# A two-layer transformer with a hybrid block on Trainium2: who splits weights and activations in the first stage

## The chip, the cores and the metric

One core of a Trainium2 chip. The metric is the device time of one execution in microseconds, as a median over runs. The engines are TensorE (PE; its weight loads are PEld), VectorE (DVE), ScalarE (ACT), GpSimd (POOL) and SyncE (SP), whose queue issues the loads and stores.

## The reference, cut to what matters

Two transformer layers, a gated mixer in the first and attention in the second, followed by a third block (mLSTM and sparse attention). Sequence 512, width 1024, float32. The change lies in the very first stage:

```python
c_act = silu(c)
mod = c_act @ ada_w[0] + ada_b[0]
sh_m, sc_m = mod[:1024], mod[1024:2048]
h = rms_norm(x, pre_mix_g[0]) * (1 + sc_m) + sh_m
z = gelu(h @ a_w_in[0] + a_b_in[0])
u, v = split(z, 2)
```

Beside it, `p @ w_ple` (the embedding for the end of the program) is computed here too.

## The kernel before

**Products in three parts.** Every matrix product is made of three passes of PE. An operand f is split into a high part (f rounded to the matmul's format) and a low part (f minus the high part), and `mm3` (L415) adds high x high, high x low and low x high: L416, L417 and L418. So each weight of 128 x 1024 that is loaded into a `raw` buffer (four of them) needs two operations in `wsplit` (L274): ACT makes the high part `whi` (L279), DVE or POOL the low part `wlo` (L282). The argument `share=1` gives the low part to POOL; without it DVE has it; `share=3` gives POOL every third of all splits, by a counter.

**The first stage** (from L595) works through the eight blocks of 128 columns of the normed x, k = 0 to 7. Its order on ACT, DVE, PE and SP is the order in which the code is written (a manual schedule); where the text below says that something stands behind something else on an engine, it can't pass it. `prep(k)` does:

- `mods(k)` (L705): two products of DVE with `cact` (silu of c, copied to all rows), each over a loaded 128 x 1024 block `d` of the modulation weights with a sum into one column of `modc` (`ada`, L302). Three operations on single columns follow: the bias on the shift (L708), the scale plus bias plus 1 (L709), and times the norm's gain, into `g0` (L710).
- the split of one weight: on even k a chunk of `w_v` (low part on POOL), on k = 1 and 3 one of `w_u` (low part on DVE).
- `to_T(k)` (L372): four transposes on PE (L384), then ACT applies scale and shift from PSUM into `t` (L407), then DVE casts `t` to the high part of h (L408) and subtracts for the low part (L409).

`products(k)` follows on PE: 12 matmuls of h against `w_v`'s chunk k/2 into four accumulators, and matmuls of `w_u` for two blocks, with some of them caught up when a block begins. `prep(k+1)` is written ahead of `products(k)`.

**Ahead of it**, the start-up: silu of c on ACT (L670), PE's copy of it to all rows (L683) and DVE's copy into `cact` (L685), the splits of `w_pl`, the squares and norms of x (L668, L656 to L664), and the embedding's products with their copies (L649, L651). The loads stand on SP in the order of the code: `crow` (which is c) first, then `pT`, `w_pl`, x, and the modulation blocks with the first `w_v` and `w_u` between them.

**Behind it** the accumulators are evacuated (`ev_v`, L764 to L766), and `gemm_b` goes on with the other three groups of `w_v`, with modulation columns for later stages in between.

## Time and profile before

| | |
|---|---|
| median of 3 runs | 1910.1 us (1907.51 to 1917.22) |
| the profiled execution | 1910.77 us, span 1908.9 us |
| PE busy | 1832.5 us, 96% of the span |
| DVE busy | 1130.9 us, 59% |
| ACT busy | 792.2 us, 41% |
| POOL busy | 375.9 us, 20% |
| granted PE clock, mean | 0.983 |

Times in the trace are microseconds from the start of the span. A row of the timeline has the start, the duration, the engine, the line, what is written and read, and in brackets how long the engine was idle before it and who ended that. In the windows view the columns are the stretch, its length, the busy time of PE, PEld, DVE, ACT and POOL with the count of instructions, the granted PE clock as a share of 2.4 GHz, the share of DMA time and the rate.

### The profile page before, as it was taken

What the parts mean: (1) busy time and instruction counts of PE and PEld (TensorE: products, weight loads), DVE (VectorE), ACT (ScalarE), POOL (GpSimd) and SP (SyncE); (2) the same over time, 40 slices, a digit from 0 to 9 for tenths busy, and PEclk for the clock granted to TensorE, in tenths of its full rate; (3) what the DMA queues carried; (4) which work ended last, traced back from release to release, by engine and by line L of the source; (5) the groups of instructions that cost most, each with busy time, mean ns of one, the idle gap of its engine ahead of it and who ended that gap; (6) DMA issues with size and microseconds to landing.
All of it is one profiled execution on the core that took longest, in us unless ns stands there. A gap on an engine that the chain in (4) does not pass through costs nothing. (4 is left out here: it accounts for less than half of the span.)

```text
span 1908.9 us, 23835 instructions
## 1 busy us (share of the span) xinstructions
PE 1832.5 (96%) x8688; PEld 1514.8 (79%) x8688; DVE 1130.9 (59%) x2132; ACT 792.2 (41%) x1395; POOL 375.9 (20%) x216
## 2 busy tenths in 40 slices
PE   8899989999999999799998999999989999999998
PEld 5788877888888877587777888888878888888887
DVE  7879844677772256439876433232267978846534
ACT  5334324423232245448764422222246246455334
POOL 2100122222220012344323111100020363031011
PEclk9999999999999999899998999999989999999999
DMA  8684752477773444855533222222434744332522
GB/s 336 235 280 134 238 207 83 158 266 271 249 253 107 136 144 145 265 177 157 185 100 111 92 97 99 97 98 103 144 116 134 231 143 135 105 105 89 192 90 100
DMA packets 109647, 305.75 MB, mean 160 GB/s; under 512 B 12277, under 2 KB 15133, under 8 KB 109530
## 3 DMA queue, kind: packets, MB, share of 16 engines
q1 hardware_dynamic: 109530, 304.23, 47.8%
q8 instruction: 69, 1.13, 0.2%
q14 instruction: 48, 0.39, 0.1%
HBM read 269.50 MB, written 37.30 MB: 161 GB/s over the span
## 5 line engine op out<-in xcount | busy, mean ns | idle before, releaser
L279 ACT ACTIVATE whi<-raw 128x1024 fp32r<-128x1024 f32 x293 | 309.9, 1059 | 672.0 <-PE acc L418 295.9
L282 POOL TENSOR_TENSOR wlo<-raw,whi 128x1024 fp32r<-128x1024 f32 x124 | 305.2, 2465 | 1348.5 <-ACT whi L279 1062.2
L417 PE MATMUL acc<-h,whi 128*128 128x512 f32 (+1 forms) x1112 | 417.3, 375 | 10.4 <-DVE h L409 10.2
L416 PE MATMUL acc<-h,whi 128*128 128x512 f32 (+1 forms) x1112 | 417.6, 376 | 5.8 <-DVE h L408 5.2
L418 PE MATMUL acc<-h,wlo 128*128 128x512 f32 (+1 forms) x1112 | 416.0, 374 | 0.6 <-POOL wlo L282 0.6
L282 DVE TENSOR_TENSOR wlo<-raw,whi 128x1024 fp32r<-128x1024 f32 x169 | 214.4, 1271 | 299.2 <-ACT whi L279 294.7
L416 PE MATMUL acc<-whi,h 128*128 128x512 f32 x608 | 241.4, 398 | 19.5 <-ACT whi L279 12.2
L417 PEld LDWEIGHTS acc<-h,whi 128*128 128x128 f32 x1112 | 212.3, 191 | 48.2 <-DVE h L409 12.7
L416 PEld LDWEIGHTS acc<-h,whi 128*128 128x128 f32 x1112 | 212.4, 191 | 42.1 <-DVE h L408 6.0
L417 PE MATMUL acc<-wlo,h 128*128 128x512 f32 x608 | 240.0, 395 | 4.8 <-DVE wlo L282 3.3
L418 PEld LDWEIGHTS acc<-h,wlo 128*128 128x128 f32 x1112 | 212.4, 191 | 37.2 <-POOL wlo L282 1.0
L418 PE MATMUL acc<-whi,h 128*128 128x512 f32 x608 | 240.2, 395 | 0.0
L416 PE MATMUL acc<-whi,s 128*128 128x512 f32 (+1 forms) x488 | 190.5, 390 | 0.7 <-DVE t L1305 0.7
L302 DVE SCALAR_TENSOR_TENSOR raw<-raw,cact 128x1024 f32<-128x1024 f32 x96 | 146.7, 1535 | 74.8 <-DMA raw<-in_ada 68.2
L417 PE MATMUL acc<-wlo,s 128*128 128x512 f32 (+1 forms) x488 | 190.7, 391 | 0.0
L418 PE MATMUL acc<-whi,s 128*128 128x512 f32 (+1 forms) x488 | 190.2, 390 | 0.0
L416 PEld LDWEIGHTS acc<-whi,h 128*128 128x128 f32 x608 | 115.2, 190 | 44.3 <-ACT whi L279 12.6
L417 PEld LDWEIGHTS acc<-wlo,h 128*128 128x128 f32 x608 | 115.2, 190 | 29.2 <-DVE wlo L282 4.1
L418 PEld LDWEIGHTS acc<-whi,h 128*128 128x128 f32 x608 | 115.2, 190 | 26.0 <-DVE h L409 3.0
L416 PEld LDWEIGHTS acc<-whi,s 128*128 128x128 f32 x488 | 91.7, 188 | 20.0 <-DVE t L1305 1.1
L417 PEld LDWEIGHTS acc<-wlo,s 128*128 128x128 f32 x488 | 91.7, 188 | 18.8
L418 PEld LDWEIGHTS acc<-whi,s 128*128 128x128 f32 x488 | 91.7, 188 | 18.8
(349 smaller groups left out, 2395.4 us busy)
## 6 DMA issues: line engine op xcount, KB each, us to landing
raw<-in_ada SPq DMA_DIRECT2D x96, 512.0 KB, 3.7
raw<-in_w_gu SPq DMA_DIRECT2D x88, 512.0 KB, 3.7
raw<-in_w_dn SPq DMA_DIRECT2D x44, 512.0 KB, 3.2
scr<-t SPq DMA_DIRECT2D x72, 256.0 KB, 3.8
raw<-in_w_o SPq DMA_DIRECT2D x20, 512.0 KB, 3.3
row<-scr SPq DMA_DIRECT2D x36, 256.0 KB, 3.3
d<-in_ada SPq DMA_DIRECT2D x16, 512.0 KB, 5.5
raw<-in_w_v SPq DMA_DIRECT2D x16, 512.0 KB, 5.1
```

The source lines that it names most:

```text
L279: S_.activation(hi[:, 0:n], raw[:, 0:n], AF.Copy)
L282: e.tensor_sub(lo[:, 0:n], raw[:, 0:n], hi[:, 0:n].bitcast(F32))
L302: V.scalar_tensor_tensor(raw, raw, 1.0, cact[0], ALU.mult, ALU.mult, accum_out=modc[:, col:col + 1])
L416: PE.matmul(out, lh, rh, start=start, stop=False)
L417: PE.matmul(out, lh, rl, start=False, stop=False)
L418: PE.matmul(out, ll, rh, start=False, stop=stop)
```

## The change

In the first stage, the high part of h is made by ACT in a second pass over the same PSUM tile (`twice`, L408 and L409 of the changed code), and DVE only subtracts (L412 there). All low parts of `w_v` go to DVE (no `share` any more). A weight is split behind h (`take(k)`) and one step earlier in the count of k than it is used: `w_v`'s chunk 0 ahead of everything, `w_u` in the steps of h0 and h2, the chunks of `w_v` in those of h1, h3 and h5. The operations on columns are two instead of three: 1 plus the bias of the scale is added once for all eight columns (`ab1`, L705 there), then one operation makes `g0` (L711) and one the shift (L712). And `crow` is loaded as the fourth load instead of the first.

```diff
@@ -369,7 +369,7 @@
             for h in range(2):
                 V.tensor_scalar_mul(out[h], xr[h], ss[:, 2:3])
 
-        def to_T(ts, xn, g, sh, hi, lo, js=range(KD), spill=None):
+        def to_T(ts, xn, g, sh, hi, lo, js=range(KD), spill=None, twice=False):
 
 
             n = len(ts) * P
@@ -405,7 +405,10 @@
                     S_.activation(fj, src, AF.Copy, scale=g[:, j:j + 1])
                 else:
                     S_.activation(fj, src, AF.Identity, scale=g[:, j:j + 1], bias=sh[:, j:j + 1])
-                V.tensor_copy(hi[j][:, c], fj)
+                if twice:
+                    S_.activation(hi[j][:, c], src, AF.Identity, scale=g[:, j:j + 1], bias=sh[:, j:j + 1])
+                else:
+                    V.tensor_copy(hi[j][:, c], fj)
                 V.tensor_sub(lo[j][:, c], fj, hi[j][:, c].bitcast(F32))
 
         def hpair():
@@ -608,13 +611,12 @@
             EVA = (0, 0)
 
             crow = L2()[0:1, :]
-            nc.sync.dma_start(crow, a["crow"])
             pf = [L(), L()]
-            wpl = []
+            wpl = [load_w(a["w_pl"][0, 0])]
             for k in range(2):
                 nc.sync.dma_start(pf[k], a["pT"][k])
-            for k in range(2):
-                wpl.append(load_w(a["w_pl"][k, 0]))
+            nc.sync.dma_start(crow, a["crow"])
+            wpl.append(load_w(a["w_pl"][1, 0]))
             xn = {}
             for t in range(NT):
                 xn[t] = [L(), L()]
@@ -699,29 +701,36 @@
                     bt = L()[0:8, 0:n]
                     V.tensor_copy(bt, pt[0:8, 0:n])
                     bts.append((bt, c0, n))
-                g0 = newg()
+                g0, ab1 = newg(), newg()
+                V.tensor_scalar_add(ab1, vc("adab", 8, 8), 1.0)
 
 
                 def mods(j, loads):
                     for col, raw in loads:
                         ada(col, raw)
+                    V.scalar_tensor_tensor(g0[:, j:j + 1], modc[:, 8 + j:9 + j], ab1[:, j:j + 1], vc("pmg0", j), ALU.add, ALU.mult)
                     V.tensor_add(modc[:, j:j + 1], modc[:, j:j + 1], vc("adab", j))
-                    V.scalar_tensor_tensor(g0[:, j:j + 1], modc[:, 8 + j:9 + j], 1.0, vc("adab", 8 + j), ALU.add, ALU.add)
-                    V.tensor_mul(g0[:, j:j + 1], g0[:, j:j + 1], vc("pmg0", j))
                 wv, uw, uaccs = {}, {}, []
                 early_w = []
 
+                def take(k):
+
+                    if k % 2:
+                        c = k // 2 + 1
+                        if c < KD // 2:
+                            wv[c] = wsplit(a["w_v"][0, c], raw=raws.get(2 * c))
+                    elif k // 2 < NU:
+                        uw[k // 2] = wsplit(a["w_u"][k // 2], alloc=L2, raw=raws.get(k + 1))
+
                 def prep(k):
+                    if k == 0:
+                        wv[0] = wsplit(a["w_v"][0, 0], raw=raws[0])
                     mods(k, ada0[k] if k in ada0 else [ada_load(col, L2() if k % 2 < ND else None) for col in (8 + k, k)])
-                    c = k // 2
-                    if k % 2 == 0:
-                        wv[c] = wsplit(a["w_v"][0, c], share=1, raw=raws.get(k))
-                    elif c < NU:
-                        uw[c] = wsplit(a["w_u"][c], alloc=L2, raw=raws.get(k))
                     if k == 0:
                         embed(0, 1)
                         embed(1, 1)
-                    to_T(range(NT), xn, g0, modc, *h, js=(k,))
+                    to_T(range(NT), xn, g0, modc, *h, js=(k,), twice=True)
+                    take(k)
                     if k == 0:
                         embed(2, 1)
                         embed(3, 1)
```

The order on DVE at the step that leads to h0 and in the first period behind it, before (`h_96` is h's high part for k = 0, `h_104` its low part, `d_148` to `d_156` are modulation blocks, `gcol` holds `g0`):

```order
L302 SCALAR_TENSOR_TENSOR d_148,modc<-d_148,cact_194 128x1024
L302 SCALAR_TENSOR_TENSOR d_150,modc<-d_150,cact_194 128x1024
L708 TENSOR_TENSOR modc<-modc,vecs 128x1
L709 SCALAR_TENSOR_TENSOR gcol<-modc,vecs 128x1
L710 TENSOR_TENSOR gcol<-gcol,vecs 128x1
L408 CAST h_96<-t_307 128x512
L409 TENSOR_TENSOR h_104<-t_307,h_96 128x512
L302 SCALAR_TENSOR_TENSOR d_154,modc<-d_154,cact_194 128x1024
L302 SCALAR_TENSOR_TENSOR d_156,modc<-d_156,cact_194 128x1024
L708 TENSOR_TENSOR modc<-modc,vecs 128x1
L709 SCALAR_TENSOR_TENSOR gcol<-modc,vecs 128x1
L710 TENSOR_TENSOR gcol<-gcol,vecs 128x1
```

and in the changed kernel (there `gcol` also holds `ab1`):

```order
L705 TENSOR_SCALAR gcol<-vecs 128x8
L282 TENSOR_TENSOR wlo_277<-raw_152,whi_276 128x1024
L302 SCALAR_TENSOR_TENSOR d_148,modc<-d_148,cact_194 128x1024
L302 SCALAR_TENSOR_TENSOR d_150,modc<-d_150,cact_194 128x1024
L711 SCALAR_TENSOR_TENSOR gcol<-modc,gcol,vecs 128x1
L712 TENSOR_TENSOR modc<-modc,vecs 128x1
L412 TENSOR_TENSOR h_104<-t_307,h_96 128x512
L282 TENSOR_TENSOR d_312<-raw_158,d_311 128x1024
L302 SCALAR_TENSOR_TENSOR d_154,modc<-d_154,cact_194 128x1024
L302 SCALAR_TENSOR_TENSOR d_156,modc<-d_156,cact_194 128x1024
L711 SCALAR_TENSOR_TENSOR gcol<-modc,gcol,vecs 128x1
L712 TENSOR_TENSOR modc<-modc,vecs 128x1
```

The low part of `w_v` (`wlo_277`) now stands ahead of the first product, the cast is gone, and the low part of `w_u` (`d_312`) stands between h0's low part and the next two products.

The order on ACT around h5 (L407 makes `t`, L279 a weight's high part; `raw_526` and `raw_494` are `w_v`'s last chunk, `raw_613`, `raw_615`, `raw_606` and `raw_608` the first two weights of the next stage), before:

```order
L407 ACTIVATE t_449<-tp_444,modc,gcol 128x512
L407 ACTIVATE t_495<-tp_490,modc,gcol 128x512
L279 ACTIVATE whi_528<-raw_526 128x1024
L407 ACTIVATE t_537<-tp_532,modc,gcol 128x512
L279 ACTIVATE whi_656<-raw_613 128x1024
L279 ACTIVATE whi_686<-raw_615 128x1024
L407 ACTIVATE t_573<-tp_568,modc,gcol 128x512
```

and in the changed kernel:

```order
L407 ACTIVATE t_445<-tp_440,modc,gcol 128x512
L409 ACTIVATE h_100<-tp_440,modc,gcol 128x512
L407 ACTIVATE t_490<-tp_485,modc,gcol 128x512
L409 ACTIVATE h_101<-tp_485,modc,gcol 128x512
L279 ACTIVATE whi_496<-raw_494 128x1024
L279 ACTIVATE whi_649<-raw_606 128x1024
L279 ACTIVATE whi_679<-raw_608 128x1024
L407 ACTIVATE t_531<-tp_526,modc,gcol 128x512
L409 ACTIVATE h_102<-tp_526,modc,gcol 128x512
```

Each `t` is followed by a high part of h (L409), and three splits of weights now stand between h5 and h6.

The first loads on SP, before:

```order
L611 DMA d_115<-in_crow 1x1024
L615 DMA s_117<-in_pT 128x512
L615 DMA s_118<-in_pT 128x512
L271 DMA raw_121<-in_w_pl 128x1024
L271 DMA raw_123<-in_w_pl 128x1024
L622 DMA s_125<-in_x 128x512
```

and in the changed kernel:

```order
L271 DMA raw_118<-in_w_pl 128x1024
L617 DMA s_116<-in_pT 128x512
L617 DMA s_117<-in_pT 128x512
L618 DMA d_115<-in_crow 1x1024
L271 DMA raw_123<-in_w_pl 128x1024
L624 DMA s_125<-in_x 128x512
```

`crow` moves behind the first `w_pl` and both halves of `pT`.

## Rows read from the trace of the kernel before

**Rows 1.** Windows: stretch, length, busy PE, PEld, DVE, ACT, POOL, clock, DMA share, GB/s.

```profile
26.66:68.39 41.73, 34.47 (x153) 25.59 (x152) 36.98 (x66) 13.17 (x16) 9.91 (x4) 1.00 0.78 290
...
72.88:150.00 77.12, 77.12 (x341) 63.74 (x340) 58.66 (x89) 28.38 (x35) 7.31 (x3) 1.00 0.74 252
```

**Rows 2.** Waits of PE, 24 to 73 us: total, times, longest.

```profile
PE acc L416 <- DVE h L408: 7.3, 4, 2.5
```

**Rows 3.** Timeline of DVE: start, duration, instruction, idle before it and releaser.

```profile
18.67 1.20 DVE L302 SCALAR_TENSOR_TENSOR d<-d,cact 128x1024 f32<-128x1024 f32 x1
...
21.06 2.22 DVE L708 TENSOR_TENSOR modc<-modc,vecs 128x1 f32<-128x1 f32 x1
...
24.60 0.43 DVE L408 CAST h<-t 128x512 fp32r<-128x512 f32 x1 [1.06 <-ACT t L407]
25.06 0.69 DVE L409 TENSOR_TENSOR h<-t,h 128x512 fp32r<-128x512 f32 x1
25.67 1.22 DVE L302 SCALAR_TENSOR_TENSOR d<-d,cact 128x1024 f32<-128x1024 f32 x1
...
28.08 0.16 DVE L708 TENSOR_TENSOR modc<-modc,vecs 128x1 f32<-128x1 f32 x1
...
28.42 1.23 DVE L282 TENSOR_TENSOR d<-raw,d 128x1024 fp32r<-128x1024 f32 x1
29.56 0.42 DVE L408 CAST h<-t 128x512 fp32r<-128x512 f32 x1
...
30.63 3.42 DVE L302 SCALAR_TENSOR_TENSOR d<-d,cact 128x1024 f32<-128x1024 f32 x1
...
36.58 0.43 DVE L408 CAST h<-t 128x512 fp32r<-128x512 f32 x1 [0.93 <-ACT t L407]
...
67.92 0.42 DVE L408 CAST h<-t 128x512 fp32r<-128x512 f32 x1
```

**Rows 4.** Timeline of POOL, the low part of a weight.

```profile
30.42 2.54 POOL L282 TENSOR_TENSOR wlo<-raw,whi 128x1024 fp32r<-128x1024 f32 x1 [7.16 <-ACT whi L279]
```

**Rows 5.** Timeline of ACT in the steps of h0 to h2.

```profile
19.47 1.06 ACT L279 ACTIVATE whi<-raw 128x1024 fp32r<-128x1024 f32 x1
...
28.62 0.78 ACT L407 ACTIVATE t<-tp,modc,gcol 128x512 f32<-128x512 f32 x1 [0.57 <-DVE gcol L710]
29.29 1.05 ACT L279 ACTIVATE whi<-raw 128x1024 fp32r<-128x1024 f32 x1
35.77 0.78 ACT L407 ACTIVATE t<-tp,modc,gcol 128x512 f32<-128x512 f32 x1 [5.43 <-DVE gcol L710]
```

**Rows 6.** Issues of the sync queue, and time to landing, first 8 us.

```profile
0.73 0.35 SPq L611 DMA_DIRECT2D d<-in_crow  x1
...
2.01 0.91 SPq L271 DMA_DIRECT2D raw<-in_w_pl  x2
...
raw<-in_w_pl SPq DMA_DIRECT2D x2, 512.0 KB, 4.7
```

**Rows 7.** Timeline of ACT in the first 10 us.

```profile
2.20 1.05 ACT L670 ACTIVATE d<-d 1x1024 f32<-1x1024 f32 x1 [0.20 <-DMA d<-in_crow]
...
6.72 1.06 ACT L279 ACTIVATE whi<-raw 128x1024 fp32r<-128x1024 f32 x1 [1.95 <-DMA raw<-in_w_pl]
8.98 1.06 ACT L279 ACTIVATE whi<-raw 128x1024 fp32r<-128x1024 f32 x1 [1.21 <-DMA raw<-in_w_pl]
```

**Rows 8.** Timeline of PE, then of DVE, in the start-up.

```profile
3.31 3.78 PE L683 MATMUL tp<-d,onec 1*128 1x512 f32 x4 [3.31 <-ACT d L670]
...
11.62 0.69 DVE L651 COPY t<-tp 128x512 f32<-128x512 f32 x1 [1.39 <-PE tp L418]
12.95 0.16 DVE L656 TENSOR_REDUCE sm<-sm 128x2 f32<-128x4 f32 x1 [0.64 <-ACT junk L668]
```

**Rows 9.** Windows with a wait of PE; the clock stands behind POOL.

```profile
19.70:22.70 3.00, 3.00 (x8) 2.30 (x7) 2.97 (x5) 1.42 (x2) 2.10 (x1) 0.50 1.03 416
...
65.00:68.40 3.40, 0.86 (x5) 0.39 (x3) 3.30 (x10) 1.44 (x2) 0.00 (x0) 1.00 0.43 157
```

## The prediction

> **What bounds the kernel now.** Read the page's first block before anything else: TensorE (PE) is busy nearly all of the span, so a change pays only where PE waits. The change sits in the first stage, so I read the windows by stage next. Up to 26.66 us the start-up runs. From 26.66 to 68.39 PE is busy 34.47 of 41.73 us, and from 72.88 to 150 it is busy 77.12 of 77.12 [rows 1]. So PE leaves the first stage with holes and enters a stretch without any: whatever moves the last piece of h, h7, moves the end by about as much. The waits view names the holes: PE waits for VectorE's high part of h, 7.3 us in four waits [rows 2]. That is the most that any relief of VectorE (DVE) can give back after 26.66; it is 0.4% of the span. Then read DVE's own rows [rows 3]. Count its time in periods, from one cast (start of h's high part) to the next: eight casts from 24.60 to 67.92, seven periods, 43.3 us. The period 24.60 to 29.56 takes 4.96 us. The next, to 36.58, takes 7.02, because the product with `cact` that starts at 30.63 takes 3.42 us instead of 1.22 (at 25.67): GpSimd (POOL) began a weight's low part at 30.42 [rows 4] and DVE stood still for it, 2.2 us. There are four such products of 3.4 us in the seven periods, and one more stall ahead of them, the column operation of 2.22 us at 21.06 against 0.16 at 28.08 [rows 3]. So POOL's help costs DVE 8.8 us between h0 and h7. In the rest of a period DVE waits for ScalarE (ACT): 0.93 us before the cast at 36.58 [rows 3].
>
> **The change part by part: one period.** Removed per period: the cast, 0.46 us (24.60 to 25.06). The three column operations, from 28.08 until ACT starts at 28.62 [rows 3, 5], take 0.54; two that don't wait for each other I put at 0.35 (one step of 0.19 less). Added: ACT makes h's high part in a second pass, which starts 0.67 us after the first (28.62 to 29.29 is ACT's pitch after such a pass [rows 5]), and DVE's low part can start only 0.81 after that (35.77 to 36.58 [rows 3, 5]). So a period without weights is: low part of h 0.61 (25.06 to 25.67), two products with their read-outs 2.41 (25.67 to 28.08), 0.35, 0.67 and 0.81: **4.85 us**. With a weight behind h it is longer. ACT splits the high part after its second pass, so it starts at +0.67 from that pass and DVE may follow 1.10 later (the spacing of 19.47 plus its 1.05 us), at +1.77; but h's low part ends at +0.81+0.61 = +1.42, so DVE waits 0.35 and then works 1.14 (28.42 to 29.56): **6.34 us**. Before, the two `w_u` low parts ran on DVE inside the wait for ACT at almost no cost; now they lie in the open.
>
> Of the seven periods four carry a weight's low part alone (4 x 6.34 = 25.4); the period between h4 and h5 and that between h6 and h7 carry none in the open (2 x 4.85 = 9.7; the next stage's low part, placed before h6, fits into ACT's pass). The one between h5 and h6 carries the last `w_v` chunk and, since POOL still makes the first low part of the next weights, one stall of 2.2: 8.5. Sum 43.6 against 43.3: **+0.3 us**. So three of the four stalls go (6.6 us) and the casts (3.2), and they come back as five low parts in the open (7.5) and seven second passes (0.67 each, 4.7), less 1.3 of column operations.
>
> **The step before h0.** Now DVE must first make the low part of `w_v`'s chunk 0. Its high part is ACT's at 19.47 [rows 5], so DVE starts it at 20.57 and the first product at 21.71 instead of 18.67: +3.04. The stall of 2.06 at 21.06 goes, the column operations give 0.2 back, the second pass costs 0.67, the cast's 0.46 go, and ACT was itself still busy for 0.1 before its pass: h0 is ready **+0.9 us** later. PE has the embedding's products until 26.66, so h0 itself hides; but DVE's chain to h7 starts there, and that doesn't.
>
> **The first loads.** `crow` moves from first to fourth on the sync queue. Before, it was issued at 0.73 and ACT took it at 2.20: 1.47 us [rows 6, 7]. Now it is issued near 2.01, where the first `w_pl` was. Lower bound of its landing: 2.01 + 1.47 = 3.5; upper bound, that of the 512 KB load issued there, 4.7 us later: 6.7 [rows 6]. ACT's order still begins with the Silu of `crow` and the table load, then the two splits. PE's copy of `crow` to all rows ended 4.9 us after the Silu's start (2.20 to 3.31 + 3.78 [rows 7, 8]); the first embedding's six products follow, about 2.3 us at the slow clock (8 in 3.00 us [rows 9]), then DVE's copy, 0.6, and only then the first norm's reduction, which stood at 12.95 [rows 8] and heads ACT's next four squares. With a landing at 6.7 that reduction starts near 14.6, +1.6; with 3.5 nothing changes, since the second `w_pl` still lands at 8.98 [rows 7], as many bytes being ahead of it. The load is queued behind 1 MB, so I take a landing near 6.3 and **+1.2 us**, between 0 and 1.6. The Trainium skill ("DMA: Bandwidth & Descriptors", section "Two DMAs through the same engine are not ordered") says that within one queue of an engine descriptors start in order; by that this term would be the upper end, 1.6, and no row here shows a small load behind large ones with its landing.
>
> Costed at nothing: the earlier load of `w_v`'s chunk 2 (a split now needs it in h3's step, some 20 us after its issue near 21); the POOL instructions removed (POOL is idle otherwise); the order of the first evacuations in the next stage, where one product with `cact` now stands ahead of the third (1.15 us, while PE reaches the bank in question some 7 us after the first); the bias copies that the sync queue issues earlier.
>
> **Sum.** +0.9 +0.3 +1.2 = +2.4 us. The profiled execution took 1910.77, so 1913.2 by it; the median of the three runs, 1910.1, lies 0.7 below it, hence 1912.5 for a median. A measurement of this kernel can tell about 0.5% (9.6 us) from no change, so this is the case "no change", a little on the slow side.
>
> **The rivals.**
> (1) The DVE low parts hide after all and the stalls are gained in full: each of the four weight periods at 4.85 instead of 6.34, so 6 us less: 1906.5; at most the 7.3 us of rows 2, 1903. For it: the stalls are real [rows 3, 4]. Against it: DVE's new order has the weight's low part strictly behind h's low part and ahead of the next products, so nothing covers it. 0.17. Even this isn't more than 0.5%.
> (2) The pieces cancel: `crow` lands early, and the sum is +1.2 or less: 1910 to 1911. 0.17.
> (3) Slower: the clock of PE. With a weight in each period PE finishes its 18 products (some 4.1 us) and then stands still for 2 us or more in nearly every period, and near 4 us before h6. After the embedding's gap the clock did fall: granted 0.50 (1.2 GHz) from 19.7 to 22.7; but the stretch 65.0 to 68.4, with a wait of 2.5 us in it, kept 1.00 (2.4 GHz) [rows 2, 9]. If it fell in every wait and stayed low, 18 products at 0.38 to 0.43 and the transposes would take 8.3 us, more than the period of 6.34: PE would be the bound, 2 us in each of seven periods, 14 in all: 1926.5. It decides only where the clock stays low for whole periods; a single fall near h6 costs some 1.3 us, which I count in the range. 0.06. The Trainium skill ("TensorE: Matmul & The Clock Gate", section "HAM oscillation — how this bites in real kernels") describes this: bursts of matmuls parted by waits, each of which begins slow again. The waits before this change disagree with it by their 1.00; the one near 4 us has no row here.
>
> **How the numbers follow.** Forecast (a loss of 1.2 to 4 us) 0.60, rivals 0.17, 0.17, 0.06. Range: down to rival 1, 1906; up to the upper bound of `crow` (+0.4), one fall of the clock (+1.3) and a scatter of runs that reached 7 us above their median, of which I take 4.8: 1919. Faster by over 0.5% needs more than all of PE's waits: 0.02. Slower by over 0.5% is rival 3: 0.06. Within 0.5%: 0.92.
>
> **What would show it.** In the changed profile: the Silu of `crow` starting at 5.5 to 6.7 instead of 2.20; h0's low part on DVE at 26 to 28; periods near 6.3 with a weight and 4.9 without; only one product of 3.4 us left between h0 and h7, in the step of h6; PE's waits moved to nearly every step, with their sum no smaller; h7's first product at 70 to 72 instead of 68.39; the rest of the kernel as it was. I am wrong if periods with a weight come near 5 us (rival 1), if Silu starts before 4 (rival 2), or if the granted clock shows 0.5 between 30 and 70 us (rival 3).

## The result and the profile after

| | before | changed |
|---|---|---|
| median of 6 runs each | 1915.85 us (1907.51 to 1917.99) | 1924.16 us (1920.64 to 1930.12) |
| ratio | | 1.0054, 95% interval 1.0036 to 1.0073 |
| the profiled execution | 1910.77 us, span 1908.9 us | 1930.12 us, span 1928.3 us |

The change costs 8 to 10 us (by the medians, by the ratio); 1912.5 was predicted, with 1906 to 1919 as the range. That number stood on the first three runs of before (median 1910.1) and a loss of 2.4; the six runs above have a median of 1915.85. The profiled execution of the changed kernel is the slowest of its six, and that of before is faster than four of its six, so their difference, 19 us, is more than twice that of the medians. What is systematic has to be found inside the traces.

**A ruler.** PE executes the same 8688 matmuls in the same order in every kernel of this study (by their count, tiles and shapes in the traces). The *lag* of a kernel at a place is the start of one such matmul in its trace less the start of the same matmul in the first trace of before. Two places are used: h7's first product, which starts at 68.39 in before, and the one that starts there at 135.07, behind the last stall of the next stage. The changed kernel's lag is 2.7 us at the first (71.09) and 11.8 at the second. At 510 us it is 12.6. So some 9 us arise between 73 and 135 us, in code that the diff doesn't touch.

The windows of the changed kernel (columns as in [rows 1]): the first stage up to h7, the next stage, and two short stretches behind PE's longest waits.

```profile
26.00:71.10 45.10, 37.65 (x157) 28.52 (x156) 32.55 (x57) 19.68 (x26) 2.49 (x1) 0.92 0.78 286
75.60:150.00 74.40, 68.02 (x287) 55.44 (x286) 49.28 (x66) 21.21 (x28) 7.38 (x3) 0.95 0.73 245
66.20:69.70 3.50, 3.50 (x10) 2.73 (x9) 1.97 (x6) 1.45 (x2) 0.00 (x0) 0.51 0.31 122
...
125.60:131.00 5.40, 5.40 (x13) 4.25 (x14) 5.40 (x8) 3.11 (x5) 0.00 (x0) 0.50 0.85 281
```

The second line is the surprise. Before, PE was busy for 77.12 of 77.12 us in this stage [rows 1]; now 6.4 us are missing. PE's waits, 24 to 73 us and then 73 to 150 us:

```profile
PE acc L419 <- ACT h L409: 7.5, 4, 2.5
...
PE acc L419 <- DVE s L773: 6.4, 2, 5.4
```

The first line answers to [rows 2] and is as large as there. The second has no counterpart before: PE waits for VectorE to evacuate an accumulator (L773, in `ev_v`). And behind the long wait, which ends at 125.57, PE runs 5.4 us at a granted clock of 0.50 (1.2 of 2.4 GHz), which costs half of them, 2.7. The sum, 6.4 + 2.7 = 9.1, is what the lag grows by between the two places, 11.8 - 2.7.

**The first stage** came out much as predicted. ScalarE's Silu of `crow`; VectorE's first norm reduction, `w_v`'s first low part and the first product; then the period from h0 to h1, the one stalled product left, h6 and h7; last, POOL's row for that stall:

```profile
5.64 1.06 ACT L672 ACTIVATE d<-d 1x1024 f32<-1x1024 f32 x1 [3.64 <-DMA d<-in_crow]
...
14.03 0.14 DVE L658 TENSOR_REDUCE sm<-sm 128x2 f32<-128x4 f32 x1
...
21.42 1.22 DVE L282 TENSOR_TENSOR wlo<-raw,whi 128x1024 fp32r<-128x1024 f32 x1 [1.12 <-ACT whi L279]
22.56 1.22 DVE L302 SCALAR_TENSOR_TENSOR d<-d,cact 128x1024 f32<-128x1024 f32 x1
...
26.70 0.69 DVE L412 TENSOR_TENSOR h<-t,h 128x512 fp32r<-128x512 f32 x1 [1.57 <-ACT h L409]
27.65 1.22 DVE L282 TENSOR_TENSOR d<-raw,d 128x1024 fp32r<-128x1024 f32 x1 [0.26 <-ACT d L279]
28.79 1.22 DVE L302 SCALAR_TENSOR_TENSOR d<-d,cact 128x1024 f32<-128x1024 f32 x1
29.93 1.22 DVE L302 SCALAR_TENSOR_TENSOR d<-d,cact 128x1024 f32<-128x1024 f32 x1
...
32.96 0.69 DVE L412 TENSOR_TENSOR h<-t,h 128x512 fp32r<-128x512 f32 x1 [1.59 <-ACT h L409]
...
58.61 3.42 DVE L302 SCALAR_TENSOR_TENSOR d<-d,cact 128x1024 f32<-128x1024 f32 x1
...
64.98 0.69 DVE L412 TENSOR_TENSOR h<-t,h 128x512 fp32r<-128x512 f32 x1 [0.43 <-ACT h L409]
...
69.73 0.69 DVE L412 TENSOR_TENSOR h<-t,h 128x512 fp32r<-128x512 f32 x1 [1.56 <-ACT h L409]
...
58.45 2.49 POOL L282 TENSOR_TENSOR wlo<-raw,whi 128x1024 fp32r<-128x1024 f32 x1 [45.80 <-ACT whi L279]
```

A period with a weight (26.70 to 32.96) takes 6.26 us. The idle time of 1.57 us ahead of the low part of h (0.43 ahead of h6's) is the wait for ACT's two passes, with nothing left to put into it; the weight's low part (27.65) lies behind it in the open.

**The next stage.** VectorE's rows of the changed kernel around the stall. Four evacuations (L773) belong to each group of `w_v`; group 0 is the one whose products end the first stage, and what is called the second group here is g = 2 in the code, the second of the three that follow. Number the products with `cact` (L302) from the start of group 0's evacuations; these are the 11th to the 14th, and then the first evacuation of the second group, for which PE waits:

```profile
110.16 1.22 DVE L302 SCALAR_TENSOR_TENSOR raw<-raw,cact 128x1024 f32<-128x1024 f32 x1 [4.14 <-DMA raw<-in_ada]
...
112.68 3.39 DVE L302 SCALAR_TENSOR_TENSOR raw<-raw,cact 128x1024 f32<-128x1024 f32 x1 [0.15 <-DMA raw<-in_ada]
...
117.17 1.23 DVE L302 SCALAR_TENSOR_TENSOR raw<-raw,cact 128x1024 f32<-128x1024 f32 x1 [1.09 <-DMA raw<-in_ada]
...
123.59 1.23 DVE L302 SCALAR_TENSOR_TENSOR raw<-raw,cact 128x1024 f32<-128x1024 f32 x1 [5.19 <-issue]
...
124.74 0.68 DVE L773 TENSOR_TENSOR s<-acc,row 128x512 f32<-128x512 f32 x1
```

The same five operations before the change, and the second pair of evacuations:

```profile
105.21 1.23 DVE L302 SCALAR_TENSOR_TENSOR raw<-raw,cact 128x1024 f32<-128x1024 f32 x1 [0.55 <-DMA raw<-in_ada]
108.47 2.98 DVE L302 SCALAR_TENSOR_TENSOR raw<-raw,cact 128x1024 f32<-128x1024 f32 x1 [2.03 <-DMA raw<-in_ada]
111.38 1.21 DVE L302 SCALAR_TENSOR_TENSOR raw<-raw,cact 128x1024 f32<-128x1024 f32 x1
...
113.66 1.27 DVE L764 TENSOR_TENSOR s<-acc,row 128x512 f32<-128x512 f32 x2
116.02 1.23 DVE L302 SCALAR_TENSOR_TENSOR raw<-raw,cact 128x1024 f32<-128x1024 f32 x1 [1.09 <-DMA raw<-in_ada]
...
118.37 1.27 DVE L764 TENSOR_TENSOR s<-acc,row 128x512 f32<-128x512 f32 x2
```

Two things differ. First the order: the 14th product stood behind the second group's first two evacuations and now stands ahead of all four. Second the loads: the 11th product waits 4.14 us for its load and the 14th stands 5.19 us after whatever VectorE did last. The sync queue shows what is new beside those loads; the changed kernel, then before:

```profile
101.74 1.54 SPq L1218 DMA_DIRECT2D scr<-scr  x1
103.38 0.54 SPq L298 DMA_DIRECT2D raw<-in_ada  x1
...
116.49 0.48 SPq L1218 DMA_DIRECT2D scr<-scr  x1
117.07 1.68 SPq L298 DMA_DIRECT2D raw<-in_ada  x2
```

```profile
100.62 0.33 SPq L298 DMA_DIRECT2D raw<-in_ada  x1
...
111.48 1.47 SPq L298 DMA_DIRECT2D raw<-in_ada  x2
113.00 0.58 SPq L1209 DMA_DIRECT2D scr<-scr  x1
```

`scr<-scr` are the bias copies, 320 KB each, from one place in HBM to another; the third block needs them, much later. Now one stands just ahead of the 11th product's load and one just ahead of the 14th's. From issue to use these loads take 110.16 - 103.38 = 6.8 and 123.59 - 117.07 = 6.5 us, against 4.6 and 4.5 before (105.21 - 100.62 and 116.02 - 111.48). So there are two theories for the 9 us, the **order** on VectorE and the **copies** on SP, and beside them the first stage (late `crow`, open low parts) and mere scatter of runs.

### The profile page after: what moved, and what is told of

It reads as the page before. It is cut to its first block, busy times and chain, and to the rows that moved or that the text cites. A ratio compares the mean times of both kernels' runs of the same rounds, so it can differ in the third digit from the quotient of the medians.

```text
span 1928.3 us, 23826 instructions
## 1 busy us (share of the span) xinstructions
PE 1839.1 (95%) x8688; PEld 1519.3 (79%) x8688; DVE 1131.0 (59%) x2121; ACT 796.3 (41%) x1403; POOL 365.9 (19%) x212
## 4 chain that ended last, share of the span: by engine, by line
PE 72%; DVE 12%; DMA 6%; ACT 3%; issue 3%; SPq 1%; POOL 0%; DVEq 0%; ACTq 0%; POOLq 0%
PE acc L419 22%; PE acc L420 22%; PE acc L421 22%; DMA raw<-in_ada 5%; DVE raw L302 2%; PE tp L1022 1%; PE tp L1007 1%; PE tp L384 1%; DVE s L1329 1%; DVE sm L1328 1%; DVE wlo L282 1%; DVE h L411 1%; ACT whi L279 1%; PE tp L824 1%; PE tp L980 1%
## 5 line engine op out<-in xcount | busy, mean ns | idle before, releaser
L279 ACT ACTIVATE whi<-raw 128x1024 fp32r<-128x1024 f32 x293 | 309.7, 1059 | 666.0 <-PE acc L421 291.0
L282 POOL TENSOR_TENSOR wlo<-raw,whi 128x1024 fp32r<-128x1024 f32 x120 | 294.9, 2462 | 1379.0 <-ACT whi L279 1174.1
L302 DVE SCALAR_TENSOR_TENSOR raw<-raw,cact 128x1024 f32<-128x1024 f32 x96 | 154.4, 1616 | 81.4 <-DMA raw<-in_ada 73.0
```

Source lines behind the costliest of these rows:

```text
L279: S_.activation(hi[:, 0:n], raw[:, 0:n], AF.Copy)
L282: e.tensor_sub(lo[:, 0:n], raw[:, 0:n], hi[:, 0:n].bitcast(F32))
L302: V.scalar_tensor_tensor(raw, raw, 1.0, cact[0], ALU.mult, ALU.mult, accum_out=modc[:, col:col + 1])
```

## The experiments

Ratios are to the kernel before, run on the same chip; the summary in one table. "14" means that the 14th product stands ahead of the second group's evacuation; "copies" whether bias copies are issued ahead of the 11th and 14th products' loads; then PE's waits from 73 to 150 us, the two lags in us, and the ratio.

| kernel | order | copies | PE waits | lag h7 | lag 135 | ratio |
|---|---|---|---|---|---|---|
| changed, first profile | 14 | both | 6.4 | 2.7 | 11.8 | 1.0054 (1.0036 to 1.0073) |
| again (changed) | 14 | both | 5.3 | 3.5 | 11.8 | 1.0048 (1.0027 to 1.0068) |
| m_crow | 14 | both | 5.0 | 1.4 | 9.2 | 1.0040 (1.0024 to 1.0057) |
| e_order | 13 | both | 3.2 | 3.1 | 6.4 | 1.0018 (1.0002 to 1.0035) |
| m_crow_order | 13 | both | 3.8 | 1.3 | 5.3 | 1.0032 (1.0019 to 1.0045) |
| e_scr | 14 | none | 3.2 | 3.3 | 6.9 | 1.0044 (1.0027 to 1.0060) |
| e_both | 13 | none | 0.3 | 3.0 | 3.2 | 1.0021 (1.0004 to 1.0037) |
| p_place | 14 | 11th | 2.3 | 3.9 | 8.1 | 1.0030 (1.0013 to 1.0048) |
| p_twice | 13 | none | 0.9 | 1.9 | 3.1 | 1.0016 (1.0001 to 1.0030) |
| p_dvelo | 13 | none | 0 | -7.1 | -7.2 | 0.9983 (0.9967 to 1.0000) |
| m_place | 13 | none | 1.7 | -7.1 | -4.9 | 0.9955 (0.9938 to 0.9972) |
| best | 13 | none | 1.1 | -8.3 | -6.9 | 0.9960 (0.9944 to 0.9976) |
| before2 (before) | 13 | none | 0.5 | 0.8 | 1.5 | |

An interval is 3 us wide to either side, so the terms of a few us are read from the lags, one profile for each kernel; how far a lag goes through to the time is a question of its own, taken up below.

### again: the changed kernel once more

No edit.

> The changed kernel once more, unaltered, with its profile. Order theory (the loss comes from the next stage, where VectorE's order now has one more product with cact ahead of the second group's evacuation): PE again waits over 4 us near 125 us for VectorE's evacuation and shows a granted clock of 0.5 behind it, and the ratio to the kernel before is 1.003 to 1.008. Scatter theory (the loss lies in the run that was profiled, in the later stages of identical order): the ratio is 0.999 to 1.003, and the lag of PE's instructions behind the kernel before, between 300 and 1900 us, differs by over 5 us from that of the first profile.

1926.41 us as the median of 10 runs. PE's waits from 73 to 150 us:

```profile
PE acc L419 <- DVE s L773: 5.3, 2, 4.7
```

The long one ends at 125.31, the clock is 0.50 behind it, and the lag at 135 us is the same 11.8. Later the two profiles differ: at 1000 us the lag is 21.1 in the first and 16.3 here. So the loss in the next stage repeats, and what comes behind it varies from profile to profile of the same kernel.

### before2: the kernel before once more

No edit.

> The kernel before once more, unaltered, for its profile alone. Its first profile took 1910.8 us where 31 later runs have a median of 1916.4. Scatter theory: this one lies nearer 1916, its PE shows waits between 500 and 600 us (weights' low parts that come late), which the first profile lacked and every other kernel's has, and its instructions lag 3 to 6 us behind the first profile's from there on, but less than 1 us up to 150 us. If those waits belong to the changed kernels, this profile has none between 500 and 600 us.

1914.66 us, and PE waits that the first profile lacked, 500 to 600 us:

```profile
PE acc L418 <- DVE wlo L282: 3.3, 3, 1.5
```

Its lag is 1.5 us at 135 (over the expected 1) and 5.9 at 600. The first profile of before is thus a lucky one: between 510 and 600 us the lag grows by 4.5 here, and by -0.3 to 6.9 in the other kernels' profiles. That stretch can't be read from single profiles; up to 510 us the two of before agree within 1.5. The clock, too, was kinder in the first profile: here it is 0.50 from 38.1 to 41.5 and from 61.9 to 65.4, behind waits of 1.9 and 2.2 us of the unaltered kernel, where the first profile kept 1.00 behind waits of 1.9 to 2.5.

### e_order: the order alone put back

```diff
-            V.scalar_tensor_tensor(raw, raw, 1.0, cact[0], ALU.mult, ALU.mult, accum_out=modc[:, col:col + 1])
+            ada_n[0] += 1
+            with behind[0] if ada_n[0] == 30 else ExitStack():
+                V.scalar_tensor_tensor(raw, raw, 1.0, cact[0], ALU.mult, ALU.mult, accum_out=modc[:, col:col + 1])
...
-                V.tensor_add(v, pt, bvr[g])
+                ev = V.tensor_add(v, pt, bvr[g])
+                if (g, t) == (2, 1):
+                    behind[0] = tc.issue_after(ev.ins if hasattr(ev, "ins") else ev)
```

The 14th product is held behind the second group's second evacuation, as it stood before.

> Order theory: with the fourteenth product with cact put behind the second group's evacuation, as it stood before the change, PE's wait of 5.4 us near 125 us goes (under 1 us left) and the 2.3 us of slow clock behind it too; the first stage stays as changed (h7's first product near 71). So 7 to 9 us less than the changed kernel: ratio to the kernel before 1.000 to 1.003. First-stage theory (the loss is the open low parts and the later loads of c, and the next stage only passes it on): no gain over the changed kernel, 1.004 to 1.007. Queue theory (the load that is late near 123 us is late because SP issues it late, whatever stands on VectorE): the wait only moves to the next group, 1.003 to 1.007.

Ratio 1.0018, inside what the order theory said; but a wait is left that it denied, and it has moved to the next pair of evacuations, as the queue theory said. PE's waits from 73 to 150 us, then VectorE:

```profile
PE acc L424 <- DVE s L778: 3.2, 2, 2.6
...
118.50 1.28 DVE L778 TENSOR_TENSOR s<-acc,row 128x512 f32<-128x512 f32 x2
122.44 1.23 DVE L307 SCALAR_TENSOR_TENSOR raw<-raw,cact 128x1024 f32<-128x1024 f32 x1 [2.65 <-issue]
```

The 14th product (here L307) now stands between the two pairs of evacuations, as before, yet its load is still late and the second pair waits behind it. After this wait of 2.6 us the clock stayed at 1.00. The lag at 135 us fell from 11.8 to 6.4: with the copies where they are, the order is worth 5.4 us of PE's time, somewhat more than half of the 9.

### p_place: the new places of the splits alone, in the kernel before

```diff
-                    c = k // 2
-                    if k % 2 == 0:
-                        wv[c] = wsplit(a["w_v"][0, c], share=1, raw=raws.get(k))
-                    elif c < NU:
-                        uw[c] = wsplit(a["w_u"][c], alloc=L2, raw=raws.get(k))
...
                     to_T(range(NT), xn, g0, modc, *h, js=(k,))
+                    take(k)
```

`take` is that of the change, with the low parts of `w_v` left on POOL (`share=1`).

> The kernel before with one part of the change alone: weights split behind h, the low parts of w_v still on POOL, everything else as before. Its VectorE order in the next stage has fourteen products with cact ahead of the second group's evacuation, as the changed kernel has. Order theory: a wait of PE of 4 to 6 us for that evacuation and a fall of the clock behind it, though the first stage has neither open second passes nor a late c: ratio 1.003 to 1.007. First-stage theory: within 2 us of the kernel before plus what its own first stage costs, 0.999 to 1.002, and no wait above 2 us in the next stage.

Ratio 1.0030, at the lower edge of the order theory's range; but the trace doesn't bear that theory out. Lag 3.9 at h7: h0's low part comes 1.1 later, two periods have a low part of `w_u` in the open behind h (casts at 25.66 and 31.62: 5.96 us against 4.96 of [rows 3]), and the last takes 8.0 instead of 7.2. Lag 8.1 at 135; PE's waits from 73 to 150 us:

```profile
PE acc L416 <- DVE s L771: 2.3, 2, 2.0
```

The long wait is 1.98 us where the order theory had 4 to 6, with a clock of 0.91 over 115 to 135 us. The new places alone bring the new order, and a copy ahead of the 11th product's load but none ahead of the 14th's: with the order and no copy there, the wait is small.

### m_place: the changed kernel with the splits ahead of h again

```diff
-                    if k == 0:
-                        wv[0] = wsplit(a["w_v"][0, 0], raw=raws[0])
                     mods(k, ada0[k] if k in ada0 else [ada_load(col, L2() if k % 2 < ND else None) for col in (8 + k, k)])
+                    c = k // 2
+                    if k % 2 == 0:
+                        wv[c] = wsplit(a["w_v"][0, c], raw=raws.get(k))
+                    elif c < NU:
+                        uw[c] = wsplit(a["w_u"][c], alloc=L2, raw=raws.get(k))
...
-                    take(k)
```

> The changed kernel without one part: the splits stand ahead of h again, with all low parts on VectorE. VectorE's order in the next stage is that of thirteen products with cact ahead of the second group's evacuation, and in the first stage its low parts lie in the wait for ACT's two passes: periods of 4.8 to 5.1 us instead of 6.26, PE work-bound in the first stage. Order theory: no wait over 2 us in the next stage; h7's first product at 62 to 66, 3 to 6 us earlier than before: ratio 0.996 to 0.999. First-stage theory (what is saved in the first stage comes back, since the loads of the next stage don't come earlier): PE waits for loads or VectorE in the next stage for what the first saved, 0.999 to 1.002.

1907.75 us, ratio 0.9955, with an interval that lies below 1: faster than both kernels. VectorE from h1's columns to h1's low part, and PE's waits from 24 to 73 us:

```profile
28.62 0.15 DVE L712 TENSOR_TENSOR modc<-modc,vecs 128x1 f32<-128x1 f32 x1
28.69 1.22 DVE L282 TENSOR_TENSOR d<-raw,d 128x1024 fp32r<-128x1024 f32 x1
30.37 0.69 DVE L412 TENSOR_TENSOR h<-t,h 128x512 fp32r<-128x512 f32 x1 [0.46 <-ACT h L409]
...
PE acc L419 <- ACT h L409: 1.3, 2, 1.0
```

The weight's low part lies in the wait for ACT's passes and leaves 0.46 us of it, where the changed kernel has 1.6 idle. The period is 4.78 us (25.59 to 30.37) instead of 6.26, h7's first product comes at 61.28, 7.1 earlier than before, and PE's waits fall from 7.5 to 1.3. So most of the loss of the change is in one part of it, the place of the splits, which brings the open low parts, the new order and the earlier copies together; the other parts, taken together, gain.

### p_dvelo and p_twice: which of the other parts gains

Both are the kernel before with one part. `p_dvelo` drops `share=1` where `w_v` is split:

```diff
-                        wv[c] = wsplit(a["w_v"][0, c], share=1, raw=raws.get(k))
+                        wv[c] = wsplit(a["w_v"][0, c], raw=raws.get(k))
```

> The kernel before with one part alone: all low parts of w_v on VectorE, at their old place ahead of h; the cast stays on VectorE and the order of the next stage is the old one. Theory (POOL's help was the loss; at the old place a low part fits into the wait for ACT): products with cact of 3.4 us between h0 and h7 fall from four to one, periods of 5.0 to 5.2 instead of 7.02 and 4.96, h7's first product at 62 to 64, ratio 0.996 to 0.998. Rival (the gain of the kernel without the new placement is that of ACT's second pass, since the cast's 0.46 us per period is what VectorE lacks): the periods stay near 6 and the ratio at 0.999 to 1.001.

`p_twice` calls `to_T` with the change's `twice=True` and nothing else.

> The kernel before with one part alone: ACT makes the high part of h in a second pass; low parts of w_v stay on POOL, the splits stay ahead of h. Theory (POOL's help was the loss): the four products of 3.4 us stay, each period loses the cast's 0.46 us and gains up to 0.8 us of waiting for the second pass, so the seven periods take 43 to 46 us against 43.3; h7's first product at 68 to 71; ratio 0.999 to 1.002. Rival (ACT's second pass is what gains): periods shorter by 0.4 us or more, 40 us in all, ratio 0.997 to 0.999.

`p_dvelo` has h7's first product at 61.28, its periods are 4.8 to 5.1 (one of 7.2, with the one stall left), and PE's waits from 24 to 73 us fall from 7.3 [rows 2] to 2.3; ratio 0.9983, a little above what was expected:

```profile
PE acc L416 <- DVE h L408: 2.3, 2, 1.7
```

`p_twice` keeps the four stalls, its seven periods take 44.0 us (26.32 to 70.31), its lag at h7 is 1.9, its ratio 1.0016. So VectorE making all low parts, without POOL beside it, gives the first stage's 7 us, and the second pass gives nothing by itself. Whether the second pass and the merged columns add something to `p_dvelo` is not settled: `m_place` and `best` are faster by 0.0023 to 0.0028, with intervals that overlap.

### best: c first as well

The `m_place` kernel, with `crow` as the first load again.

```diff
             crow = L2()[0:1, :]
+            nc.sync.dma_start(crow, a["crow"])
...
-            nc.sync.dma_start(crow, a["crow"])
```

> The changed kernel without two parts: the splits stand ahead of h again, and c is loaded first again. What is left of the change: all low parts on VectorE, ACT's second pass, the merged column operations. Theory: Silu of c at 2.2 instead of 5.6 to 6.4, the first norm's reduction 1.1 to 1.9 us earlier than with the late load, and the whole start-up with it; PE's first stage is bound by its own work, so h7's first product comes 0.5 to 1.5 us earlier than in the kernel with splits ahead and c late; ratio 0.994 to 0.998, which a timing can't tell from 0.9955, the trace can. Rival (the start-up waits for x and the modulation blocks, not for c): the reduction is earlier, but h0 is not.

1907.41 us, ratio 0.9960. ScalarE's Silu, and the window of the first stage:

```profile
2.12 1.05 ACT L673 ACTIVATE d<-d 1x1024 f32<-1x1024 f32 x1
...
26.00:60.13 34.13, 32.81 (x151) 25.57 (x149) 29.92 (x55) 17.07 (x23) 3.10 (x1) 1.00 0.96 367
```

PE is busy 32.81 of 34.13 us up to h7, which comes 1.2 earlier than in `m_place`; as expected the timing doesn't show this. There is little left to gain in this stage.

### m_crow and m_crow_order: the late c taken out

`crow` first, as in the diff above, in the changed kernel (`m_crow`) and with the order put back as well (`m_crow_order`).

> The changed kernel without one part: c is loaded first again; splits behind h and the order of the next stage stay as changed. Theory (the late c costs the start-up 1.1 to 1.9 us, the order of the next stage 5 to 6): Silu of c at 2.2, the first norm's reduction at 12.9 to 13.7, h7's first product 1 to 2 us earlier than in the changed kernel (69 to 70.5); the wait of PE near 124 us stays above 3.5 us, with the clock at 0.5 behind it; ratio 1.003 to 1.006. Rival (the late c shifts VectorE's ring of loads, and so makes that wait): the wait falls under 2 us and the ratio to 1.000 to 1.002.

> The changed kernel with c loaded first again and the fourteenth product with cact behind the second group's evacuation: what is left of the change against the kernel before is the first stage alone (predicted +0.9 ahead of h0, +0.3 in the periods). Theory: h7's first product at 69 to 70.5, PE's wait near 120 us at 1 to 3 us, ratio 0.9995 to 1.002, 1 to 2 us below the kernel with the order alone put back (1.0018). Rival (the late c costs nothing, h0 waits for other loads): the same as that kernel, h7 at 71, 1.0018 or more.

The lag at h7 is 1.4 and 1.3, where the five profiles with the late `crow` and splits behind h have 2.7 to 3.5 (`e_order` 3.1, `e_scr` 3.3, `e_both` 3.0 among them): by these profiles the late `crow` costs 1.3 to 2.2 us at h7. The start-up itself varies by as much: the first norm's reduction starts at 12.6 to 14.2 in the eight profiles with `crow` first and at 13.6 to 14.8 in the six with it late, 1.0 apart by the means. The late `crow` doesn't make the wait in the next stage, which is 4.01 us in `m_crow`, with the clock at 0.83 over 115 to 135 us, and 3.06 in `m_crow_order`. The second kernel's ratio, 1.0032, is above what was expected (up to 1.002), though its lag at 135 is only 5.3; the intervals of this ratio and of `e_order`'s overlap.

### e_scr and e_both: the copies taken away from the loads

```diff
-                nc.sync.dma_start(rows[g], a["wsT"][g])
+                ld = nc.sync.dma_start(rows[g], a["wsT"][g])
+                if not holdc:
+                    holdc.append(tc.issue_after(ld.ins if hasattr(ld, "ins") else ld))
...
-            for hd in range(8):
-                nc.sync.dma_start(bscr2[hd].rearrange("(p m) -> p m", p=P), bscr[hd:hd + 1, :].broadcast_to((P, 640)))
+            with holdc[0]:
+                for hd in range(8):
+                    nc.sync.dma_start(bscr2[hd].rearrange("(p m) -> p m", p=P), bscr[hd:hd + 1, :].broadcast_to((P, 640)))
```

`e_scr` is the changed kernel with this edit, `e_both` has `e_order`'s edit too. With `changed` and `e_order` they make a square: order 14 or 13, copies beside the loads or not.

> The changed kernel with the bias copies (scr to scr, 320 KB each) held on SP behind the loads of the next stages' weights, out of the stretch from 90 to 130 us; the fourteenth product with cact stays ahead of the second group's evacuation, only a weight's low part stands beside it too. Bias-copy theory (the copies, which SP now issues from 101.7 on instead of 113.0, slow the loads beside them, so that the product's loads land late): the load for the eleventh product lands in 4.5 us instead of 6.8, PE's wait near 124 us falls from 5 to under 1.5 us, no slow clock behind it, ratio 1.000 to 1.0025, what the first stage costs. Order theory (the loads are late since four buffers are handed round in VectorE's order): the wait stays above 4 us and the ratio at 1.004 to 1.006.

> The same, and the fourteenth product with cact behind the second group's first evacuations, as in the kernel with the order alone put back. Bias-copy theory: PE's wait of 2.6 to 3.1 us that was left there falls under 1 us, ratio 1.000 to 1.0025. Order theory: the same wait of 2 to 3 us as with the order alone put back, 1.002 to 1.003. If the copies only collide and do not decide: between, a wait of 1 to 2 us.

In `e_scr` the 11th and the 14th product, and PE's waits from 73 to 150 us:

```profile
107.13 1.23 DVE L304 SCALAR_TENSOR_TENSOR raw<-raw,cact 128x1024 f32<-128x1024 f32 x1 [0.79 <-DMA raw<-in_ada]
...
119.44 1.23 DVE L304 SCALAR_TENSOR_TENSOR raw<-raw,cact 128x1024 f32<-128x1024 f32 x1 [3.81 <-issue]
...
PE acc L421 <- DVE s L775: 3.2, 3, 2.1
```

Their loads were issued at 103.41 and 114.93: 3.7 and 4.5 us instead of 6.8 and 6.5. The waits fell to half, the longest to 2.1 and not under 1.5: neither theory alone is right. Here a weight's low part (1.2 us at 120.59) also stands between the 14th product and the evacuation, as in no other of these kernels, so this cell may show some 1 us too much (an estimate from that row). With both edits nothing of the wait is left:

```profile
PE acc L426 <- DVE s L780: 0.3, 1, 0.3
```

The lag grows between h7 and 135 us by 9.1 (changed; 8.3 in `again`, 7.8 in `m_crow`), 3.4 (order put back; 4.0 in `m_crow_order`), 3.6 (copies held) and 0.2 (both). With either gone the clock stays at 1.00 from 115 to 135 us. So the two act together: a late load, and an evacuation that had to wait for it.

In the time of the whole kernel the square doesn't close. `e_scr` has 1.0044, as the order theory said, and isn't told from the changed kernel (1.0048, 1.0054); `e_both` has 1.0021 against 1.0018 of `e_order`. So holding the copies gained nothing that the runs can tell. Something may be lost again behind 135 us, where the copies now stand (issued from 143 to 153 in `e_both`): both kernels that hold them show a wait of PE between 135 and 220 us (1.3 and 1.0) that no other kernel has, and by 450 us their lags have grown by 5.5 and 3.5, the others' by -0.1 to 2.8. What each of these comes from was not followed up. That the copies make the wait at 125 us is shown; that they cost time at the end is not.

## Why the prediction was wrong, point by point

- **What bounds the kernel** (PE leaves a stage with holes and enters one without, so that h7's start moves the end): right for the first stage, and the square shows that the next stage can be kept whole (0.2). But that a stage without holes has no reserve against new ones wasn't asked of the trace.
- **One period.** 6.34 with a weight was predicted and 6.26 measured, 4.85 and 4.78, 8.5 and 8.46. The seven take 43.0 instead of 43.3: -0.3 for +0.3. VectorE's rows gave the sum within 0.6 us. The recount by parts that follows that sum in the prediction doesn't agree with it: 7.5 + 4.7 - 1.3 against 6.6 + 3.2 is +1.1, not +0.3.
- **The step before h0.** +0.9 predicted. h0's low part starts at 26.70 against 25.06 [rows 3]; less the 1.1 of the start-up (the reduction at 14.03 against 12.95 [rows 8]) that is +0.6.
- **The first loads.** `crow` reached ScalarE at 5.64, and between 5.2 and 6.4 in the other profiles with this order, 3.1 to 4.3 us after its issue behind the larger loads; alone at the head it took 1.47 [rows 6, 7]. +1.2 was predicted and up to 1.6 allowed; the reduction's start gives 1.1 here and 1.0 by the means of all profiles, the lags 1.3 to 2.2. The Trainium skill ("DMA: Bandwidth & Descriptors", section "Two DMAs through the same engine are not ordered") has descriptors start in order within one queue of one DMA engine; these landings agree: `crow` is taken behind the landings of the first `w_pl` (4.2 to 4.8) and of the first half of `pT` (4.8 to 5.5) in all six. The upper end that was worked out from it was not reached here, 1.1 against 1.6, though three of the other profiles come to 1.7 to 1.9.
- **Rival 3, the clock.** It did fall in the first stage, from 45.8 to 49.2 and near h6 (0.51 from 66.2 to 69.7), behind waits of 1.8 and 1.9 us and not behind one of 2.5; the wait before h6 that was put near 4 us took 1.9 here and 3.3 in the six other profiles with the splits behind h and all their low parts on VectorE. The prediction's sign for this rival, a clock of 0.50 between 30 and 70 us, came, but it comes in `before2` as well, so it can't tell the change from its absence; and the 1.00 behind the waits of the first profile, which the prediction set against a fall, isn't what every run of that kernel shows. h7's low part starts 1.36 us later than before (69.73 against 68.37), but PE's first product with h7 2.7 later: PE was still at h6's products at half speed. This is the 1.3 us that the range held for a single fall. PE didn't become the bound over whole periods, which is what the rival's 14 us needed. What it missed is a fall in the next stage.
- **Rival 1** fell here (no period with a weight came near 5 us), for the reason given against it. With the splits ahead of h, in `m_place`, it is just what happens.
- **The step that failed** is the sentence "Costed at nothing", in two of its items. "The order of the first evacuations in the next stage": it was read for the first few evacuations alone and priced as one product of 1.15 us. The move that counted lies 50 us later, where the 14th product passes the second group's evacuation; and what it brings to the evacuation isn't its 1.15 us but the wait for its load. "The bias copies that the sync queue issues earlier": they stand just ahead of loads that VectorE is waiting for, and make them 2 to 3 us later (6.8 and 6.5 against 3.7 and 4.5). Each gives some 5 us of PE's time at 135 us when it is undone (11.8 to 6.4 and to 6.9), the two 8.6 (to 3.2). Neither had a bound in the range.
- **The base.** "The median of the three runs, 1910.1" is a term of the sum, too, and was 5.7 too small: six runs give 1915.85, and 20 to 31 later ones 1914.1 to 1916.4. Of the 11.7 us between 1912.5 and 1924.16, some 6 are this base and some 6 the loss that was costed at nothing (8.3 by the medians against 2.4). On the later base the same loss would be 1918.3.
- **The sum of the first stage**, +2.4 for a measured lag of 2.7, is right in part by luck. VectorE's chain, which it adds up, brought +1.4 (1.1 + 0.6 - 0.3: h7's low part at 69.73 against 68.37); the other 1.3 is the fall of the clock near h6, which the sum left to the range. In the four other profiles with the late `crow` and splits behind h the chain brings 1.0 to 2.2, under the forecast each time, and the lag is 3.0 to 3.5.

What stays open: how much of a lag at 135 us is left at the end, and so how the 8 to 10 us of the medians divide between the order, the copies and the first stage. The lags of `p_dvelo` and `m_place` and their ratios stand in the opposite order, and between 510 and 600 us profiles of one kernel differ by as much as 4.5 us.

## What to carry to other kernels

A change in one stage reorders the next where a scheduler decides: compare the order of every engine as far as the stretch without waits reaches, and ask of each operation that now stands ahead of an evacuation not how long it takes but when its load lands. On a queue that is kept short by a few buffers, a copy that nobody needs yet isn't free if it is issued ahead of a load that somebody waits for; whether holding it back pays has to be seen in the time, which here it didn't show. A base of three runs, with a lucky one profiled, can be off by more than the loss that is forecast. And a low part is free only in a wait: ahead of h it lay beside ScalarE's passes (4.78 us a period), behind h in the open (6.26).

## What the runs showed of the hardware

A copy of 320 KB within HBM delays the 512 KB load issued right behind it on the same queue. The 14th product's load shows it clearly: 6.0 to 6.6 us from issue to use in the five profiles with a copy 0.6 us ahead of it, 4.4 to 4.9 in the nine without; a copy issued 1.1 us behind it (`p_place`: 116.05 to 120.49) left it at 4.4. For the 11th the ranges overlap: 5.5 to 6.8 in the six profiles with a copy 0.8 to 1.6 us ahead, 3.7 to 5.9 in the eight without, and 3.7 where the copies were held away.

PE's clock in the next stage stayed at 1.00 after waits of 2.1, 2.6 and 3.1 us and was 0.50 behind those of 4.0, 4.7 and 5.4. But in `p_place` it fell near a wait of 1.98, and in the first stage of `before2` behind waits of 1.9 and 2.2 where the first profile of the same kernel kept 1.00 behind 1.9 to 2.5. So the length of a wait alone doesn't tell in these runs whether the clock falls.
